# Rounding the high half of each weight tile on the scalar engine instead of on GpSimd, in a two-layer hybrid decoder trunk

## The chip, the cores and the metric

The kernel runs on one core of a Trainium2 chip. The metric is the device time of one execution in microseconds. The engines are named as in the profile: PE (TensorE, the matrix products), PEld (its weight loads), DVE (VectorE), ACT (ScalarE), POOL (GpSimd) and SP (SyncE, which issues the transfers here).

## The reference

Two layers; in each, one input projection feeds three groups of heads (differential attention, dilated attention, a Mamba-2 scan), one output projection joins them, and a gated MLP follows. Everything is float32.

```python
for layer in range(DEPTH):                       # DEPTH = 2, SEQ = 1024, D_MODEL = 1024
    h = rms_norm(x, pre_mix_norm[layer])
    proj = h @ w_in[layer]
    dq, dk, dv, lq, lk, lv, z, xbc, dt = jnp.split(proj, IN_OFFSETS, axis=-1)
    ...
    o_diff = diff_attention(dq, dk, dv, lam, diff_head_norm[layer], lambda_init)
    o_dil = dilated_attention(lq, lk, lv)
    o_ssd = ssd_mixer(z, xbc, dt, ...)
    mix = jnp.concatenate([o_diff, o_dil, o_ssd], axis=-1) @ w_out[layer]
    x = x + rms_norm(mix, post_mix_norm[layer])
    h = rms_norm(x, pre_ffn_norm[layer])
    u = causal_dwconv(h @ ffn_up[layer], ffn_conv_w[layer], ffn_conv_b[layer])
    g, val = jnp.split(u, [D_FF], axis=-1)       # D_FF = 2816
    f = (jax.nn.silu(g) * val) @ ffn_down[layer]
    x = x + rms_norm(f, post_ffn_norm[layer])
```

## The kernel before

Every dense product is made in three passes of a shorter float format (fp32r in the profile). Each operand is split into a high half, the value rounded to that format, and a low half, the rest: hi·hi, hi·lo and lo·hi are added up in one PSUM accumulator. The activations are split once (ah and al, or g for the gated product); the weights are split tile by tile as they come from memory, in `wsplit`: SP loads a tile `wr` of 128x1024 float32 (three buffers; the last, odd piece of a down-projection group is 128x512), one engine writes the rounded copy `wh`, DVE subtracts to get `wl` (four buffers each). So a `wh` can be written when its tile has landed and when the matmuls that read the buffer four tiles earlier are done; `wl` needs `wh`; and `wr` is free for the next load when `wl` is written. There are 390 such tiles in the two layers.

`mm3` (L200 to 211) multiplies weights that stand in the array's place of stationary data (wh, wl) with 512 columns of activations: the parts of the input projection that are wanted transposed, and the FFN's up-projection. `tm3` (L148 to 159), with `tm_units`, has the activations stationary and the weights moving: the rest of the input projection (wtm), the output projection (wout), the down-projection (wdn). Three PSUM accumulators named acc take turns; ACT or DVE empties them (L361 in the causal convolutions, L774 to L777 after wtm, L793 and L794 after wout, L840 and L842 after wdn).

The program goes through each layer in this order: input projection for the first half of the rows with the first attention heads woven in, then for the second half with the rest of the attention and the scan; output projection of the first half; FFN of the first half, with the mixer of the second half woven in; the second half's output projection; its FFN; the norms between. The norm's factor is made in `rstd` (L114 to L123): two small DVE operations, a power on POOL (`rs_r`, L115), and on DVE two or three more (L118 and L119, or L121 to L123); then L243 scales a whole row tile by it. A framework sorts the instructions into each engine's queue by its own estimates of their times and dependencies, with hints from the code (high priority; issue after a given matmul). Each queue then runs in the order so found, and the semaphores between engines follow from the tiles.

Of the kernel before, what the change touches and what calls it, by code (L numbers as in the profile page):

```python
# [13 lines left out]
AF = mybir.ActivationFunctionType  # L14
ALU = mybir.AluOpType
# [54 lines left out]
def body(ctx, tc, x_in, win, wtm, wdt, wout, wup, wdn, cst, gains, dtb, alog, lamp, kst, rope, out):  # L70
    nc = tc.nc
    P = 128
# [6 lines left out]
    V, A, G, T_, Y = nc.vector, nc.scalar, nc.gpsimd, nc.tensor, nc.sync  # L79
# [26 lines left out]
    def fr(ap):  # L106
        return ap.bitcast(F32)
# [17 lines left out]

    xsrc = [x_in[t] for t in range(8)]

    E_ = dict(lo=V)

    def wsplit(src, nk):  # L130
        raw = sp.tile([P, KT * P], F32, tag="wr", bufs=3, name="wr")
        Y.dma_start(raw[:, :nk * P].rearrange("p (a n) -> p a n", a=src.shape[1]) if len(src.shape) == 3 else raw[:, :nk * P], src)
        hi = sp.tile([P, KT * P], F32R, tag="wh", bufs=4, name="wh")
        lo = sp.tile([P, KT * P], F32R, tag="wl", bufs=4, name="wl")
        G.tensor_scalar(hi[:, :nk * P], raw[:, :nk * P], 1.0, 0.0, op0=ALU.mult, op1=ALU.add)  # L135
        E_["lo"].tensor_tensor(lo[:, :nk * P], raw[:, :nk * P], fr(hi[:, :nk * P]), op=ALU.subtract)  # L136
        return hi, lo

    hold = [None]
# [21 lines left out]
    def tm_units(w, k0, nk, pair, evac, before=None, inner=False, pairs=0):  # L161

        def tiles(c):
            return [(i, min(2, nk - i)) + wsplit(w[c, :, k0 + i:k0 + min(i + 2, nk)], min(2, nk - i) * 4)
                    for i in range(0, nk, 2)]
# [132 lines left out]
    for l in range(NL):  # L298
# [118 lines left out]
        def in_unit(name, Ts):  # L417
            hi, lo = wsplit(win[l, IN_IDX[name]], KT)
            for T in Ts:
                a = acc()  # L420
                mm3(a, hi, lo, rhs_of(hT[T]), KT)
                in_evac(name, T, a)
# [379 lines left out]
        def up_pair(T, j, pair):  # L802
            us = []
            for q in range(2):
                jj = j + 22 * q
                hi, lo = wsplit(wup[l, jj], KT)
                a = acc()
                mm3(a, hi, lo, rhs_of(pair), KT)
                u = t2("cv", 4)
                conv(a, u, 3, fw[:, jj], ustate[:, jj], T)  # L810
                us.append(u)
                if q == 0:
                    th = t2("cv", 4)
                    A.activation(th[:], u[:], AF.Tanh)
                    V.scalar_tensor_tensor(u[:], th[:], 1.0, u[:], op0=ALU.add, op1=ALU.mult)
                    yield
            u, w = us
            V.tensor_tensor(u[:], u[:], w[:], op=ALU.mult)
            gh = t2("g", 12, F32R)
            gl = t2("g", 12, F32R)  # L820
            A.activation(gh[:], u[:], AF.Copy)
            V.tensor_tensor(gl[:], u[:], fr(gh[:]), op=ALU.subtract)  # L822
            gt[j] = (gh[:], gl[:])
            yield
# [3 lines left out]
        def down_group(T, gi, fT):  # L828
            k0, n = GROUPS[gi]
            last = gi == len(GROUPS) - 1  # L830
            f = [fT[:, 2 * t:2 * t + 2].rearrange("p k n -> p (k n)") for t in range(4)]
            if last and T:
                xs = load_x(T)
                g3 = load_gain(l, 3)
                g0 = load_gain(l + 1, 0) if l < NL - 1 else None

            def evac(c, t, a):
                d = slice(c * H, (c + 1) * H)
                if gi == 0:
                    A.activation(f[t][:, d], a[:], AF.Copy)  # L840
                else:
                    V.tensor_tensor(f[t][:, d], a[:], f[t][:, d], op=ALU.add)  # L842
                if last and T and l == NL - 1:
                    if c == 0:
                        fin.append((rows(), tiny()))
                    r, sq = fin[-1]
                    A.activation(r[:, d], f[t][:, d], AF.Square, accum_out=sq[:, c:c + 1])
                    if c == 1:
                        V.tensor_tensor(sq[:, 0:1], sq[:, 0:1], sq[:, 1:2], op=ALU.add)
                        rs = rstd(sq[:, 0:1], 1, 1.0 / DM, EPS)  # L850
                        for d in (slice(0, H), slice(H, DM)):
                            V.scalar_tensor_tensor(r[:, d], f[t][:, d], rs[:, 0:1], g3[:, d], op0=ALU.mult, op1=ALU.mult)
                            E = G if d.start == 0 else V
                            E.tensor_tensor(r[:, d], xs[t][:, d], r[:, d], op=ALU.add)
                            Y.dma_start(out[4 * T + t, :, d], r[:, d])
                elif last and T and c == 1:
                    fin.append(fin_norm(4 * T + t, xs[t], f[t], g3, g0))
            return tm_units(wdn[l], k0, n, [gt[k0 + k] for k in range(n)], evac, inner=last and T == 1)
# [108 lines left out]
        dense, rs = out_units(1, pair)  # L967
        run(dense)
        hold[0] = lastmm[0]
        E_["lo"] = V  # L970
        dense = down_group(0, NG - 1, fT0)
        hp = follow(dense, 1, rs, (1, 2, 2, 3))
        run(dense)
        hold[0] = None
        E_["lo"] = V
        fT1 = sp.tile([P, KT, H], F32, tag="act", bufs=4, name="fT")
        dense = ffn(1, hp, fT1)
        half = fin_half(fT0)
# [98 lines left out]
```

## Time and profile before

| | |
|---|---|
| time, median of 3 runs | 2744.13 us (2742.87 to 2744.74) |
| the profiled execution | 2745.8 us, of which its span is 2743.9 |
| granted TensorE clock, mean | 0.988 |
| busy in the span: PE | 2649.0 us (97%) |
| DVE | 1885.0 us (69%) |
| ACT | 883.0 us (32%) |
| POOL | 721.5 us (26%) |
| the copy wh, L135 on POOL | 390 times, 464.4 us |
| the subtraction wl, L136 on DVE | 390 times, 479.1 us |

Busy time is the time in which an instruction of the engine ran; the rest of the span the engine waited. "Idle before" names what ended a wait. [...]

### The profile page before, as it was taken

Reading aid. Unit: us, or ns where it says so; the run is one execution under the profiler, and the core shown is the slowest. Engines: PE = TensorE matmul, PEld = TensorE weight load, DVE = VectorE, ACT = ScalarE, POOL = GpSimd, SP = SyncE. Lnnn points to the kernel's source line nnn. Section 1 sums busy time; section 2 is a strip of 40 time slices with the busy share of each in tenths; the row PEclk is TensorE's granted clock in tenths of the full one; section 3 lists DMA queues with packets and bytes.
Section 4 is the critical chain, followed back from the end, with each engine's and each line's share of the span. In section 5 each row is a group of like instructions: output and inputs, shape, how many; then the busy total and the mean of one; then the engine's idle time right before and its main releaser. Section 6 shows DMA issues by size and latency. Waiting matters only on the chain. (4 is left out here: it accounts for less than half of the span.)

```text
span 2743.9 us, 36451 instructions
## 1 busy us (share of the span) xinstructions
PE 2649.0 (97%) x13160; PEld 2147.8 (78%) x13160; DVE 1885.0 (69%) x3814; ACT 883.0 (32%) x1777; POOL 721.5 (26%) x634
## 2 busy tenths in 40 slices
PE   7999889999999999999999999899999999999998
PEld 6887677888788877888878776778887888788886
DVE  5666867556887686666775677575678775966667
ACT  3252333444432223111223533334444322321111
POOL 2301343232124222222133023332221332322222
PEclk9999999999999999999999999999999999999999
DMA  6653545443333454333257535453434334533332
GB/s 226 216 171 101 180 139 181 119 120 112 104 128 110 130 172 154 96 97 99 88 170 235 152 99 184 125 176 105 126 112 117 119 115 126 200 118 94 100 93 69
DMA packets 157348, 368.83 MB, mean 134 GB/s; under 512 B 18032, under 2 KB 53744, under 8 KB 157168
## 3 DMA queue, kind: packets, MB, share of 16 engines
q1 hardware_dynamic: 157168, 366.49, 42.8%
q8 instruction: 105, 1.72, 0.3%
q14 instruction: 75, 0.61, 0.1%
HBM read 306.13 MB, written 60.29 MB: 134 GB/s over the span
## 5 line engine op out<-in xcount | busy, mean ns | idle before, releaser
L135 POOL TENSOR_SCALAR wh<-wr 128x1024 fp32r<-128x1024 f32 (+1 forms) x390 | 464.4, 1193 | 1390.6 <-PE acc L207 786.8
L204 PE MATMUL acc<-ah,wh 128*128 128x512 f32 x1952 | 776.3, 398 | 1.5 <-ACT ah L255 1.5
L207 PE MATMUL acc<-al,wh 128*128 128x512 f32 x1952 | 765.8, 392 | 0.5 <-DVE al L256 0.5
L208 PE MATMUL acc<-ah,wl 128*128 128x512 f32 x1952 | 764.7, 392 | 0.0
L136 DVE TENSOR_TENSOR wl<-wr,wh 128x1024 fp32r<-128x1024 f32 (+1 forms) x390 | 479.1, 1231 | 251.5 <-POOL wh L135 248.4
L204 PEld LDWEIGHTS acc<-ah,wh 128*128 128x128 f32 x1952 | 368.1, 189 | 82.6 <-issue 10.2
L208 PEld LDWEIGHTS acc<-ah,wl 128*128 128x128 f32 x1952 | 368.1, 189 | 77.4 <-issue 0.5
L207 PEld LDWEIGHTS acc<-al,wh 128*128 128x128 f32 x1952 | 368.1, 189 | 75.1 <-issue 2.7
L363 DVE SCALAR_TENSOR_TENSOR cv<-acc,cs,cv 128x511 f32<-128x511 f32 (+2 forms) x436 | 323.5, 742 | 14.0 <-ACT cv L361 12.2
L154 PE MATMUL acc<-wh,g 128*128 128x512 f32 x704 | 283.1, 403 | 7.6 <-DVE cv L369 6.5
L361 ACT ACTIVATE cv<-acc,cs 128x512 f32<-128x512 f32 x204 | 158.8, 779 | 390.7 <-PE acc L208 379.9
L157 PE MATMUL acc<-wl,g 128*128 128x512 f32 x704 | 276.9, 395 | 6.7 <-DVE wl L136 3.4
L158 PE MATMUL acc<-wh,g 128*128 128x512 f32 x704 | 275.2, 394 | 0.3 <-DVE g L822 0.3
L597 DVE CUSTOM_DVE_ANT_0 P<-s,kc 128x512 f32<-128x512 f32 (+3 forms) x224 | 130.2, 587 | 151.3 <-PE s L595 145.3
L157 PE MATMUL acc<-wl,ah 128*128 128x512 f32 x512 | 208.7, 408 | 16.1 <-DVE wl L136 16.1
L600 ACT ACTIVATE P<-P,tiny 128x128 f32<-128x128 f32 (+7 forms) x224 | 173.3, 774 | 158.4 <-DVE tiny L599 135.3
L154 PE MATMUL acc<-wh,ah 128*128 128x512 f32 x512 | 206.6, 405 | 4.1 <-POOL wh L135 2.4
L158 PE MATMUL acc<-wh,al 128*128 128x512 f32 x512 | 205.9, 402 | 1.8 <-DVE al L256 1.8
L154 PEld LDWEIGHTS acc<-wh,g 128*128 128x128 f32 x704 | 133.1, 189 | 44.7 <-issue 13.1
L157 PEld LDWEIGHTS acc<-wl,g 128*128 128x128 f32 x704 | 133.4, 190 | 33.4 <-DVE wl L136 8.0
L158 PEld LDWEIGHTS acc<-wh,g 128*128 128x128 f32 x704 | 133.3, 189 | 30.0 <-DVE g L822 2.4
L842 DVE TENSOR_TENSOR fT<-acc,fT 128x512 f32<-128x512 f32 x160 | 108.4, 684 | 68.9 <-PE acc L158 68.8
(183 smaller groups left out, 3184.5 us busy)
## 6 DMA issues: line engine op xcount, KB each, us to landing
wr<-in_wup SPq DMA_DIRECT2D x176, 512.0 KB, 3.5
wr<-in_wdn SPq DMA_DIRECT2D x80, 512.0 KB, 3.5
wr<-in_win SPq DMA_DIRECT2D x54, 512.0 KB, 4.4
wr<-in_wtm SPq DMA_DIRECT2D x32, 512.0 KB, 4.9
wr<-in_wout SPq DMA_DIRECT2D x32, 512.0 KB, 4.0
xd<-t SPq DMA_DIRECT2D x24, 512.0 KB, 3.0
t<-xd SPq DMA_DIRECT2D x24, 512.0 KB, 4.3
t<-in_x SPq DMA_DIRECT2D x16, 512.0 KB, 5.4
```

The lines of the kernel that those rows point to most:

```text
L135: G.tensor_scalar(hi[:, :nk * P], raw[:, :nk * P], 1.0, 0.0, op0=ALU.mult, op1=ALU.add)
L136: E_["lo"].tensor_tensor(lo[:, :nk * P], raw[:, :nk * P], fr(hi[:, :nk * P]), op=ALU.subtract)
L154: i = T_.matmul(a[:], xh, hi[:, w], start=(n0 + k == 0), stop=False)
L157: T_.matmul(a[:], xh, lo[:, w], start=False, stop=False)
L158: lastmm[0] = T_.matmul(a[:], xl, hi[:, w], start=False, stop=(n0 + k == n - 1))
L204: i = T_.matmul(a[:], hi[:, w], xh, start=(k == 0), stop=False)
L207: T_.matmul(a[:], hi[:, w], xl, start=False, stop=False)
L208: i = T_.matmul(a[:], lo[:, w], xh, start=False, stop=(k == nk - 1))
L361: A.activation(u[:], a[:], AF.Identity, scale=w[:, n:n + 1], bias=w[:, taps:taps + 1])
L363: V.scalar_tensor_tensor(u[:, d:], a[:, :H - d], w[:, n - d:n - d + 1], u[:, d:], op0=ALU.mult, op1=ALU.add)
L597: V.tensor_tensor_reduce(p[:, c:c + n], s[:, :n], mask[:, o:o + n], 1.0, -1e30 if c == 0 else mx[:, e], ALU.add, ALU.max, mx[:, e])
L600: A.activation(p[:, :nk * P], p[:, :nk * P], AF.Exp, scale=scale, bias=nm[:, e], accum_out=den[:, e])
```

## The change

The copy that rounds a weight tile to `wh` is an activation with the function Copy on ACT instead of a multiply-add by 1 and 0 on POOL. The subtraction goes to DVE by name; before, it went through a small table `E_` that always said DVE. Lines after the table's stand two earlier in the new file (L135 becomes L133, L793 becomes L791), and four earlier at its end.

```diff
-    E_ = dict(lo=V)
-
     def wsplit(src, nk):
...
-        G.tensor_scalar(hi[:, :nk * P], raw[:, :nk * P], 1.0, 0.0, op0=ALU.mult, op1=ALU.add)
-        E_["lo"].tensor_tensor(lo[:, :nk * P], raw[:, :nk * P], fr(hi[:, :nk * P]), op=ALU.subtract)
+        A.activation(hi[:, :nk * P], raw[:, :nk * P], AF.Copy)
+        V.tensor_tensor(lo[:, :nk * P], raw[:, :nk * P], fr(hi[:, :nk * P]), op=ALU.subtract)
         return hi, lo
...
-        E_["lo"] = V
```

The order of the queues follows. On POOL, at the end of the first layer's output projection for the second half of the rows (the stretch around 977 us), the powers of the norms (rs_r) stood between copies. Before:

```order
L115 TENSOR_TENSOR rs_r_8788<-rs_m_8787,kc_69 128x1
L115 TENSOR_TENSOR rs_r_8803<-rs_m_8802,kc_69 128x1
L135 TENSOR_SCALAR wh_8920<-wr_8918 128x1024
L135 TENSOR_SCALAR wh_8926<-wr_8924 128x512
L135 TENSOR_SCALAR wh_9006<-wr_9004 128x1024
L115 TENSOR_TENSOR rs_r_8841<-rs_m_8840,kc_69 128x1
```

Now:

```order
L115 TENSOR_TENSOR rs_r_8788<-rs_m_8787,kc_69 128x1
L115 TENSOR_TENSOR rs_r_8803<-rs_m_8802,kc_69 128x1
L115 TENSOR_TENSOR rs_r_8841<-rs_m_8840,kc_69 128x1
L115 TENSOR_TENSOR rs_r_8856<-rs_m_8855,kc_69 128x1
L115 TENSOR_TENSOR rs_r_8894<-rs_m_8893,kc_69 128x1
```

The three copies have left POOL's row, and nothing has come in their place. On ACT at the same place stand the squares of the norm (P from t4, L240), the evacuations of the output projection (P from acc, L793, and the square of acc, L794) and the halves of the next activations (ah, L255). Before:

```order
L793 ACTIVATE P_8612<-acc_8759 128x512
L794 ACTIVATE acc_8759,tiny_8613<-acc_8759 128x512
L240 ACTIVATE P_8612,tiny_8800<-t4_8676 128x1024
L793 ACTIVATE P_8666<-acc_8812 128x512
L794 ACTIVATE acc_8812,tiny_8667<-acc_8812 128x512
L793 ACTIVATE P_8670<-acc_8865 128x512
L794 ACTIVATE acc_8865,tiny_8671<-acc_8865 128x512
L255 ACTIVATE ah_8941<-tr_8943 128x4x128
L255 ACTIVATE ah_8941<-tr_8950 128x4x128
```

Now:

```order
L791 ACTIVATE P_8612<-acc_8759 128x512
L792 ACTIVATE acc_8759,tiny_8613<-acc_8759 128x512
L238 ACTIVATE P_8612,tiny_8800<-t4_8676 128x1024
L791 ACTIVATE P_8666<-acc_8812 128x512
L792 ACTIVATE acc_8812,tiny_8667<-acc_8812 128x512
L133 ACTIVATE wh_8920<-wr_8918 128x1024
L133 ACTIVATE wh_8926<-wr_8924 128x512
L133 ACTIVATE wh_9006<-wr_9004 128x1024
L791 ACTIVATE P_8670<-acc_8865 128x512
L792 ACTIVATE acc_8865,tiny_8671<-acc_8865 128x512
L133 ACTIVATE wh_9012<-wr_9010 128x512
L253 ACTIVATE ah_8941<-tr_8943 128x4x128
```

Three copies stand ahead of the last evacuation and its square, and a fourth ahead of the ah. At the start of the program, ACT has the squares of the first norms and the first ah. Before:

```order
L240 ACTIVATE P_101,tiny_105<-t4_96 128x1024
L240 ACTIVATE P_102,tiny_120<-t4_118 128x1024
L255 ACTIVATE ah_94<-tr_160 128x4x128
L255 ACTIVATE ah_94<-tr_167 128x4x128
L240 ACTIVATE P_103,tiny_174<-t4_156 128x1024
```

Now:

```order
L238 ACTIVATE P_101,tiny_105<-t4_96 128x1024
L238 ACTIVATE P_102,tiny_120<-t4_118 128x1024
L133 ACTIVATE wh_134<-wr_132 128x1024
L253 ACTIVATE ah_94<-tr_160 128x4x128
L133 ACTIVATE wh_140<-wr_138 128x1024
L253 ACTIVATE ah_94<-tr_167 128x4x128
L133 ACTIVATE wh_146<-wr_144 128x1024
L238 ACTIVATE P_103,tiny_174<-t4_156 128x1024
```

The first copies stand before the first ah and between the two.

## Rows read from the trace of the kernel before

**Rows 1.** The page: busy us of each engine, share, instructions.

```profile
PE 2649.0 (97%) x13160; PEld 2147.8 (78%) x13160; DVE 1885.0 (69%) x3814; ACT 883.0 (32%) x1777; POOL 721.5 (26%) x634
```

**Rows 2.** The page's groups: busy, mean ns of one | idle before, and its releaser.

```profile
L135 POOL TENSOR_SCALAR wh<-wr 128x1024 fp32r<-128x1024 f32 (+1 forms) x390 | 464.4, 1193 | 1390.6 <-PE acc L207 786.8
L136 DVE TENSOR_TENSOR wl<-wr,wh 128x1024 fp32r<-128x1024 f32 (+1 forms) x390 | 479.1, 1231 | 251.5 <-POOL wh L135 248.4
```

**Rows 3.** Windows: length, busy PE, PEld, DVE, ACT, POOL; granted clock, DMA share, GB/s.

```profile
240.00:460.00 220.00, 198.25 (x960) 155.57 (x959) 161.45 (x373) 76.71 (x203) 76.23 (x62) 0.95 0.48 152
960.00:1060.00 100.00, 89.50 (x398) 72.45 (x397) 86.19 (x160) 31.14 (x57) 26.76 (x31) 0.98 0.50 166
1060.00:1360.00 300.00, 299.86 (x1327) 246.26 (x1326) 195.77 (x309) 61.56 (x92) 66.51 (x55) 0.99 0.32 100
1360.00:1420.00 60.00, 55.45 (x248) 44.93 (x247) 46.20 (x71) 14.64 (x28) 16.94 (x18) 0.97 0.53 178
1600.00:1820.00 220.00, 198.45 (x950) 155.56 (x949) 160.96 (x372) 75.51 (x199) 76.25 (x62) 0.95 0.47 150
2330.00:2420.00 90.00, 83.66 (x368) 67.94 (x366) 80.52 (x140) 27.40 (x49) 24.95 (x27) 0.96 0.58 196
...
sum 690.00, PE 625.31 PEld 496.44 DVE 535.32 ACT 225.40 POOL 221.13; mean PE 125.06 PEld 99.29 DVE 107.06 ACT 45.08 POOL 44.23
```

**Rows 4.** Timeline around 978 us: start, length, instruction [idle before <-releaser].

```profile
977.30 2.65 POOL L135 TENSOR_SCALAR wh<-wr 128x1024 fp32r<-128x1024 f32 x3
977.36 1.00 DVE L118 SCALAR_TENSOR_TENSOR rs_q<-rs_r,rs 128x1 f32<-128x1 f32 x1 [0.60 <-POOL rs_r L115]
...
978.39 0.55 DVE L119 SCALAR_TENSOR_TENSOR rs_r<-rs_q,rs_r 128x1 f32<-128x1 f32 x1
...
978.98 2.04 DVE L243 SCALAR_TENSOR_TENSOR P<-t,rs_r,gb 128x1024 f32<-128x1024 f32 x1
...
981.01 1.21 DVE L136 TENSOR_TENSOR wl<-wr,wh 128x1024 fp32r<-128x1024 f32 x1
...
982.28 0.71 PE L157 MATMUL acc<-wl,g 128*128 128x512 f32 x1 [3.38 <-DVE wl L136]
```

**Rows 5.** One line's instructions: ns min/median/max, first and last start.

```profile
L118 DVE SCALAR_TENSOR_TENSOR rs_q<-rs_r,rs x64: 204/220/1076, 6.8 to 2737.1; 128x1 f32<-128x1 f32 x64
...
L119 DVE SCALAR_TENSOR_TENSOR rs_r<-rs_q,rs_r x64: 142/159/992, 7.1 to 2737.4; 128x1 f32<-128x1 f32 x64
...
L243 DVE SCALAR_TENSOR_TENSOR P<-t,rs_r,gb x33: 746/1284/2067, 7.3 to 2364.5; 128x1024 f32<-128x1024 f32 x31, 128x512 f32<-128x512 f32 x2
```

**Rows 6.** Timeline around 440 us: two DVE instructions and the matmul behind them.

```profile
436.37 0.99 DVE L118 SCALAR_TENSOR_TENSOR rs_q<-rs_r,rs 128x1 f32<-128x1 f32 x1 [0.30 <-POOL rs_r L115]
...
438.53 2.07 DVE L243 SCALAR_TENSOR_TENSOR P<-t,rs_r,gb 128x1024 f32<-128x1024 f32 x1
...
443.12 0.79 PE L157 MATMUL acc<-wl,ah 128*128 128x512 f32 x1 [2.78 <-DVE wl L136]
```

**Rows 7.** Timeline of PE: the matmuls behind two other pauses.

```profile
341.43 0.63 PE L684 MATMUL tr<-kc,on 128*128 128x128 f32 x4 [2.05 <-DVE on L679]
...
391.80 0.63 PE L530 MATMUL s<-P,gtr 128*128 128x384 f32 x1 [2.11 <-POOL P L504]
```

**Rows 8.** Timeline of DVE: the first and the last of 66 instructions.

```profile
259.47 1.24 DVE L456 SCALAR_TENSOR_TENSOR dtv<-cv 128x24 f32<-128x24 f32 x1
...
2413.49 1.01 DVE L369 SCALAR_TENSOR_TENSOR cv<-ustate,cs,cv 128x2 f32<-128x2 f32 x1
```

**Rows 9.** Groups by shape, ACT: a square of a 128x1024 tile from SBUF.

```profile
L240 ACT ACTIVATE P<-t 128x1024 f32<-128x1024 f32 x32 | 33.9, 1060 | 58.8 <-DVE t L272 51.5 <-DMA t<-in_x 7.0 <-DVE rs_r L119 0.2
```

**Rows 10.** The five stretches again, L135 alone: 23 + 16 + 10 + 23 + 16 copies.

```profile
240.00:460.00 220.00, 29.38 (x23) 0.95 0.48 152
...
sum 690.00, POOL 105.66; mean POOL 21.13
```

**Rows 11.** Who waited for the loads of wr (us, times), and the part for wup.

```profile
  POOL wh L135: 63.1, 23
...
POOL wh L135 <- DMA wr<-in_wup: 28.1, 8, 14.3
```

More of the change, by code (lines that the diff above doesn't have):

```diff
@@ L974, in body @@
         hold[0] = None
-        E_["lo"] = V
         fT1 = sp.tile([P, KT, H], F32, tag="act", bufs=4, name="fT")
```

## The prediction

> **What bounds the kernel now.** I read the page's line of busy times first [rows 1]: PE is busy 2649.0 us of a span of 2743.9, so some 95 us are all that a faster neighbour can give back, plus what the clock loses. The copy that the change moves is the largest item on POOL [rows 2]: 390 of them, 464.4 us of POOL's 721.5, 1193 ns each. POOL itself is at 26%, so its load is not the point.
>
> Next, the stretches in which PE is not full [rows 3]. The up-projection of the FFN is (299.86 of 300.00 us): nothing done beside it can matter. Five stretches, which hold the attention's and the SSD's ends, the output projections and the changes between norms, are not: of 690.00 us PE is busy 625.31, so 64.7 us lie idle there, two thirds of all there is. [...]
>
> Then the pauses one by one. In the one of 3.38 us before 982.28 [rows 4], PE waits for wl, and wl stands on DVE behind three instructions that took longer than they usually do. While POOL runs three wh copies from 977.30, L118 takes 1.00 us, L119 0.55 and L243 2.04; their medians are 0.22, 0.16 and 1.28 [rows 5]. All three read two tiles in SBUF. L118 starts at 977.36, just behind the copies, and is done at 978.36, which is the length of one copy later. The excess is 0.78 + 0.39 + 0.76 = 1.93 us of the pause's 3.38. The pause of 2.78 us before 443.12 [rows 6] is alike: wl stands behind an L118 of 0.99 and an L243 of 2.07, with an excess of 0.77 + 0.79 = 1.56. The pauses of 2.05 and 2.11 us [rows 7] have no such copy in their chains: the first runs through a slow rs_r of the norm, the other ends on POOL's own P of L504. They stay.
>
> So what the copies cost on POOL is time on DVE, and the change takes POOL out of DVE's way.
>
> **The change, part by part.**
>
> *What goes.* In the four pauses read closely, 1.93 + 1.56 = 3.49 us of 3.38 + 2.78 + 2.05 + 2.11 = 10.32 is hold-up by the copies, 34%. Of 64.7 us that is 22. The other way of counting: for each DVE instruction that overlaps a wh copy I took its time less the tenth percentile of its line and shape. In the five stretches 66 instructions exceed that by over 0.25 us, 48.9 us in all; the first is an L456 of 1.24 us, the last an L369 of 1.01 [rows 8]. About half should lie on PE's path, since the rest is made good while DVE waits for others: 24. I take **-23**. The ends are 0 (DVE runs into the next wait) and -49 (every hold-up counts in full). In the FFN the same hold-ups (L822 beside wh, for instance) cost nothing, because PE is full.
>
> [...]
>
> *The clock.* [...] I take **-4**, ends 0 and -10.
>
> *What comes.* The copy has no row on ACT. The nearest is the square of L240 on ACT, the same 128x1024 from SBUF: 1060 ns [rows 9]. So 390 copies make about 410 us and ACT goes from 883.0 to about 1290 us, 47% of the span: not a bound. In the five stretches there are 88 copies [rows 10], 93 us more on the 225.40 that ACT is busy there. ACT then runs a copy 13% of the time. Any of the 536 ACT instructions of the stretches (203 + 57 + 28 + 199 + 49) meets one with that chance and loses half of 1.06 us: 536 x 0.13 x 0.53 = 37 us, spread over all. Of this a tenth or so, as PE's idle share there (64.7 of 690), falls into chains that PE waits for: 4. I double it for the copies that themselves wait in ACT's queue: **+8**, ends 0 and +37. The order by which the scheduler has put them (the ACT rows shown with the change) sets three of them at the place of [rows 4] between the second and the third evacuation L793, ahead of the two L255 that prepare a next product.
>
> *The start.* There ACT runs the copies between the norms' first operations; the first products need both. **+1**, ends 0 and +2 (two operations of 1.06).
>
> *What moves.* POOL's rs_r (L115) no longer stand behind wh; in the rows shown they follow each other directly. Both were late only by DVE's doing, so I count this at nothing of its own; DVE's wait for rs_r is covered in the -23. The subtraction wl stays on DVE. SP's loads keep their order, and wr is freed by wl as before. The E_ table always said DVE and costs nothing.
>
> *The sum.* The profiled execution took 2745.8 us (1.9 more than its span, 1.7 more than the median of 2744.13). 2745.8 - 23 - 4 + 8 + 1 = 2727.8; less 1.7 that is **2726** beside the median.
>
> **The rivals.**
>
> (1) *No gain.* DVE, set free, only comes earlier to waits that the copies don't make: rs_r, P of L504, the transposes. For it: two of the four pauses [rows 7] are of this kind. Against it: the other two end on a wl that stood in line with nothing else late. Then about -5 is left: 2741 to 2742, within 0.2%.
>
> (2) *Slower, by ACT's queue.* On POOL a waiting copy hurt nobody: it sat 786.8 us for one of its buffer's readers alone [rows 2], and 63.1 us in 23 waits for the transfer of wr [rows 11]. On ACT whatever stands behind it waits too: the evacuations L793 and L361 that free PE's accumulators, the exponentials of L600, the ah of the next product. The buffer waits were foreseen by the scheduler's order, late transfers were not. One of them costs 63.1 / 23 = 2.7 us. To eat up the 18 us of gain, seven of the 23 must fall where PE has no other product; with twelve, 32 us come back and the time is 2758. Against it: most loads are early, and eight of the 23 waits, 28.1 us, were for loads of the up-projection [rows 11], where PE is full. [...]
>
> (3) *The hold-up is not POOL's.* If the copy's reads held DVE up from whichever engine, -23 and -4 fall away and +9 stays: 2753. Against it: L118's end fits the end of one copy on POOL [rows 4].
>
> **How the numbers follow.** Forecast 0.68, (1) 0.15, (2) 0.13, (3) 0.04. What a measurement of this kernel can tell from no change is about 0.2%, 5.5 us: the forecast is faster, (1) the same, (2) and (3) slower. The forecast's own range goes to -36 for the hold-up (half way to its end) with no price on ACT, 2744 - 36 - 4 + 1 = 2705, and upward into (1). The whole range goes further up to 2752, short of (2) and (3) in full: 2705 to 2752.
>
> **What would show it.** POOL's line falls to about 257 us, ACT's rises to about 1290, with 390 copies of about 1.06 us. L118, L119 and L243 on DVE fall to means near their medians; wl's mean falls below its 1231 ns. The five stretches, by the same work and not by the same clock time, have less PE idle: about 40 us instead of 64.7. If the step is wrong, DVE's means fall and PE's idle time stays (rival 1), or PE's waits end on ACT's evacuations with a wh before them that waits for wr (rival 2), or the DVE means don't fall (rival 3). A start that is late by more than 2 us would be a mis-sized term only.

## The result: faster by 46 us, and more than was forecast

The changed kernel takes 2697.8 us (median of four runs, 2694.39 to 2698.24) against 2743.5 of the kernel before in the same comparison: a ratio of 0.9834, with a 95% interval of 0.9817 to 0.9851. The forecast was 2726 with a range from 2705: the sign and the place were right, the size was less than half of what came. The medians leave out one execution of one kernel below, which ran at a granted clock of 0.568 and took 4368.56 us.

The page of the changed kernel first: busy times, and the copy and the subtraction, which answer to [rows 1] and [rows 2].

```profile
PE 2625.3 (97%) x13160; PEld 2135.6 (79%) x13160; DVE 1830.1 (68%) x3814; ACT 1246.8 (46%) x2167; POOL 252.4 (9%) x244
...
L134 DVE TENSOR_TENSOR wl<-wr,wh 128x1024 fp32r<-128x1024 f32 (+1 forms) x390 | 470.5, 1209 | 264.1 <-ACT wh L133 259.8
L133 ACT ACTIVATE wh<-wr 128x1024 fp32r<-128x1024 f32 (+1 forms) x390 | 403.9, 1040 | 432.9 <-PE acc L205 254.4
```

POOL lost 469 us of work and ACT took 364 (its instructions overlap by some 0.1 us, since the copies alone make 403.9: the one that starts at 966.71 takes 1.05 us, and the next instruction starts at 967.66). The span is 2695.8 us, so PE is idle for 2695.8 - 2625.3 = 70.5 us instead of 94.9. Its busy time fell by 23.7 us too, although it does the same 13160 matmuls. Most of that is the clock, whose mean rose from 0.988 to 0.994: what it misses of 1, times the span, was 32.9 us and is 16.2, so 16.7 less. The other 7 us are not explained. In the trace's record of the granted clock, a share of the full one, stand two levels, 1.0 and 0.5; the lower one comes 16 times in the kernel before and 9 times in the changed one, 12 and 8 of them for 3.4 us each.

The five stretches of [rows 3], now. The windows below hold the same matmuls (found by counting them from the start), not the same times. Columns: length, busy time of PE, PEld, DVE, ACT and POOL with instruction counts, granted clock, DMA share, GB/s.

```profile
239.10:444.70 205.60, 192.70 (x960) 152.10 (x960) 148.64 (x373) 99.00 (x226) 46.29 (x39) 0.98 0.51 164
947.90:1042.00 94.10, 87.92 (x397) 71.21 (x396) 80.28 (x162) 46.59 (x75) 9.59 (x15) 1.00 0.56 185
1341.70:1396.60 54.90, 53.46 (x248) 44.03 (x247) 39.97 (x71) 24.44 (x38) 5.38 (x8) 1.00 0.56 192
1574.50:1777.10 202.60, 189.76 (x950) 150.13 (x949) 148.15 (x372) 97.72 (x222) 46.02 (x39) 0.98 0.51 164
2287.40:2373.00 85.60, 82.01 (x367) 66.63 (x366) 73.61 (x140) 42.10 (x65) 7.97 (x11) 0.98 0.60 206
sum 642.80, PE 605.85 PEld 484.11 DVE 490.65 ACT 309.84 POOL 115.26; mean PE 121.17 PEld 96.82 DVE 98.13 ACT 61.97 POOL 23.05
```

They took 690.00 us and take 642.80: 47.2 us of the 48.1 by which the span fell. PE's idle time in them went from 64.7 to 37.0, by 27.7 us. The clock's missing parts times the lengths made 11.0 + 2.0 + 1.8 + 11.0 + 3.6 = 29.4 us and now make 4.1 + 0 + 0 + 4.1 + 1.7 = 9.9, by 19.5 less. PE's busy time in them fell from 625.31 to 605.85, by 19.5 us as well, for the same matmuls; so here the clock explains what the pauses don't. 27.7 + 19.5 = 47.2: pauses and clock together are the whole gain, three parts to two.

One pause as it was and is. This is the timeline around the first pause read closely, [rows 4], in the changed kernel: start, length, engine, line, instruction, and in brackets the idle time before it.

```profile
964.52 0.55 POOL L115 TENSOR_TENSOR rs_r<-rs_m,kc 128x1 f32<-128x1 f32 x1 [4.54 <-DVE rs L116]
...
965.11 0.22 DVE L118 SCALAR_TENSOR_TENSOR rs_q<-rs_r,rs 128x1 f32<-128x1 f32 x1 [0.61 <-POOL rs_r L115]
...
965.24 2.52 ACT L133 ACTIVATE wh<-wr 128x1024 fp32r<-128x1024 f32 x3
...
965.36 0.16 DVE L119 SCALAR_TENSOR_TENSOR rs_r<-rs_q,rs_r 128x1 f32<-128x1 f32 x1
...
965.56 1.28 DVE L241 SCALAR_TENSOR_TENSOR P<-t,rs_r,gb 128x1024 f32<-128x1024 f32 x1
...
967.08 1.22 DVE L134 TENSOR_TENSOR wl<-wr,wh 128x1024 fp32r<-128x1024 f32 x1
...
968.35 0.50 PE L155 MATMUL acc<-wl,g 128*128 128x512 f32 x1 [1.51 <-DVE wl L134]
```

The three copies run at the same place, now on ACT, for 2.52 us. Beside them L118 takes 0.22 us (it took 1.00), L119 0.16 (0.55) and L241, the former L243, 1.28 (2.04). The pause is 1.51 us instead of 3.38: shorter by 1.87, where the prediction had counted 1.93 of hold-up. Over the whole kernel no L118 is late any more:

```profile
L118 DVE SCALAR_TENSOR_TENSOR rs_q<-rs_r,rs x64: 209/220/223, 6.7 to 2689.3; 128x1 f32<-128x1 f32 x64
```

Its longest is 223 ns, against 1076 in [rows 5].

### The profile page after: what moved, and what is told of

It reads as the page before. It is cut to its first block, busy times and chain, and to the rows that moved or that the text cites. A ratio compares the mean times of both kernels' runs of the same rounds, so it can differ in the third digit from the quotient of the medians.

```text
span 2695.8 us, 36379 instructions
## 1 busy us (share of the span) xinstructions
PE 2625.3 (97%) x13160; PEld 2135.6 (79%) x13160; DVE 1830.1 (68%) x3814; ACT 1246.8 (46%) x2167; POOL 252.4 (9%) x244
## 5 line engine op out<-in xcount | busy, mean ns | idle before, releaser
L134 DVE TENSOR_TENSOR wl<-wr,wh 128x1024 fp32r<-128x1024 f32 (+1 forms) x390 | 470.5, 1209 | 264.1 <-ACT wh L133 259.8
L133 ACT ACTIVATE wh<-wr 128x1024 fp32r<-128x1024 f32 (+1 forms) x390 | 403.9, 1040 | 432.9 <-PE acc L205 254.4
L115 POOL TENSOR_TENSOR rs_r<-rs_m,kc 128x1 f32<-128x1 f32 (+2 forms) x88 | 66.0, 754 | 1337.6 <-DVE rs L116 1326.8
```

What stands on the lines that cost most here:

```text
L133: A.activation(hi[:, :nk * P], raw[:, :nk * P], AF.Copy)
L134: V.tensor_tensor(lo[:, :nk * P], raw[:, :nk * P], fr(hi[:, :nk * P]), op=ALU.subtract)
```

## Experiments: does POOL's reading do it?

Theory A is the prediction's: an instruction on DVE with two inputs in SBUF waits while POOL reads SBUF for the copy; PE pauses behind it, and the clock falls behind the pause. Theory B: the gain comes from POOL's queue, in which powers and other work stood behind copies. Theory C: it comes from the order that the scheduler found this time, and from the shorter copy (a mean of 1040 ns against 1193). Two kernels tell them apart. Both keep the copy on ACT and give POOL 390 needless instructions that write the wl buffer before DVE does. In one they read wr, in the other they read nothing. The orders of the DVE instructions of these two are nearly the same (3797 of 3814 stand in the same order).

```diff
-        A.activation(hi[:, :nk * P], raw[:, :nk * P], AF.Copy)
+        A.activation(hi[:, :nk * P], raw[:, :nk * P], AF.Copy); G.tensor_scalar(lo[:, :nk * P], raw[:, :nk * P], 1.0, 0.0, op0=ALU.mult, op1=ALU.add)
```

> The changed kernel (copy on ACT), and beside it POOL copies the same wr tile with the old multiply-add into the wl buffer, which DVE then overwrites: POOL reads SBUF again as often and as long as before, but nothing that wh needs goes through POOL. Theory A (POOL's reads hold DVE's two-input instructions up, PE's pauses follow and the clock falls behind the pauses): 2730 to 2748 us, PE idle back to about 90 us, mean clock 0.988, L118's mean above 300 ns. Theory B (what was won is POOL's queue, in which rs_r and others stood behind wh): about 2740 too, but then the same for the next kernel, which fills POOL without reading. Theory C (the order that the scheduler found, and the shorter copy, 1058 against 1217 ns): within 5 us of 2698.

And the one that only writes:

```diff
-        A.activation(hi[:, :nk * P], raw[:, :nk * P], AF.Copy)
+        A.activation(hi[:, :nk * P], raw[:, :nk * P], AF.Copy); G.memset(fr(lo[:, :nk * P]), 0.0)
```

> The changed kernel, and beside it POOL writes zeros into the wl buffer before DVE overwrites it: the same number of POOL instructions of the same size at the same places, in front of the same rs_r, but they read nothing. Theory A: 2695 to 2706 us (a few us at the start, where four of them stand before the first rs_r), L118's mean near 220 ns, mean clock 0.993. Theory B: as the kernel whose POOL reads, some 2740. Theory C: 2698.

The first took 2738.09 us (0.998 of before, 0.9971 to 0.9989), the second 2689.06 (0.9804, 0.9789 to 0.9819): 49 us apart. First the kernel whose POOL reads: the page's line of busy times,

```profile
PE 2642.5 (96%) x13160; PEld 2143.6 (78%) x13160; DVE 1906.3 (70%) x3814; ACT 1243.1 (45%) x2167; POOL 719.1 (26%) x634
```

and the views of two lines, POOL's needless instructions and L118 (ns min/median/max):

```profile
L133 POOL TENSOR_SCALAR wl<-wr x390: 618/1056/2125, 10.7 to 2711.3; 128x1024 fp32r<-128x1024 f32 x187, 128x512 fp32r<-128x512 f32 x8
...
L118 DVE SCALAR_TENSOR_TENSOR rs_q<-rs_r,rs x64: 203/220/1019, 8.5 to 2732.1; 128x1 f32<-128x1 f32 x64
```

Then the kernel whose POOL only writes, its busy times,

```profile
PE 2621.8 (98%) x13160; PEld 2133.8 (79%) x13160; DVE 1829.3 (68%) x3814; ACT 1245.9 (46%) x2167; POOL 618.2 (23%) x634
```

and the same two lines:

```profile
L133 POOL MEMSET wl<- x390: 522/956/969, 0.7 to 2661.6; 128x1024 f32 x187, 128x512 f32 x8
...
L118 DVE SCALAR_TENSOR_TENSOR rs_q<-rs_r,rs x64: 206/219/222, 12.2 to 2682.5; 128x1 f32<-128x1 f32 x64
```

POOL is nearly as full in both, with as many instructions in front of the same powers. Where it reads, DVE is busy 77 us longer for the same work, L118 takes up to 1019 ns, PE is idle 96.4 us and the time is within 0.2% of the old one. Where it only writes, nothing of this happens. That speaks for A and against the other two: B asks for the same time in both, C for 2698 in both. (The second kernel came out 6 us below the range expected of it, see the end.) So beside POOL instructions that only write L118 is not held up: 222 ns at most, against 1019.

How long is one hold-up? The same kernel as the first, with POOL reading only half the columns:

```diff
-G.tensor_scalar(lo[:, :nk * P], raw[:, :nk * P], 1.0, 0.0, op0=ALU.mult, op1=ALU.add)
+G.tensor_scalar(lo[:, :nk * H // 8], raw[:, :nk * H // 8], 1.0, 0.0, op0=ALU.mult, op1=ALU.add)
```

> As the kernel in which POOL copies each wr tile into the wl buffer beside ACT, but only the first half of its columns: POOL reads as often, half as long. If a DVE instruction with two SBUF inputs waits for the whole of POOL's instruction, the hold-ups are half as long: L118's longest near 0.7 us instead of 1.02, and the time between the two kernels of that pair, 2705 to 2722 (2689 with none, 2738 with all). If any read of POOL, short or long, costs the same, 2730 to 2740.

It took 2720.14 us (0.9911, 0.9896 to 0.9926), and its L118 and POOL rows (ns min/median/max) are

```profile
L118 DVE SCALAR_TENSOR_TENSOR rs_q<-rs_r,rs x64: 206/220/620, 7.0 to 2711.8; 128x1 f32<-128x1 f32 x64
...
L133 POOL TENSOR_SCALAR wl<-wr x390: 404/622/2035, 9.9 to 2690.7; 128x512 fp32r<-128x512 f32 x187, 128x256 fp32r<-128x256 f32 x8
```

The median of POOL's instruction fell from 1056 to 622 ns, to 59%; of the 49 us 31 are left, 63%; the longest L118 is 620 ns, about one such instruction. The two shares prove little by being alike. DVE's busy time fell further, from 77 us above that of the kernel whose POOL only writes to 21 (1850.3 against 1829.3), and this kernel's DVE order differs from the pair's in some 120 places of 3814. What shows the length is the single hold-up, here the longest L118 and what POOL ran beside it:

```profile
1378.06 0.62 POOL L133 TENSOR_SCALAR wl<-wr 128x512 fp32r<-128x512 f32 x1
1378.06 0.62 DVE L118 SCALAR_TENSOR_TENSOR rs_q<-rs_r,rs 128x1 f32<-128x1 f32 x1 [0.44 <-POOL rs_r L115]
```

L118 stands beside POOL's instruction and ends with it. So do all L118 and L119 of over 300 ns: each ends within 10 ns of the end of a POOL instruction that reads a wr tile, 21 of them in the kernel before, 21 where POOL reads the whole tile, 15 where it reads half. In the changed kernel and where POOL only writes there is none. The hold-up lasts until the POOL instruction beside it is done.

One more rival has to go. In the kernels of the pair DVE's subtraction must also wait until POOL has written the wl buffer: 158.8 us in 132 waits where POOL reads, 142.1 us in 113 where it doesn't. Perhaps the first is slow by these waits alone. With half the columns they are 41.3 us in 53, less than in either, and still that kernel is 31 us slower than the one that only writes. They are not the cause.

## Experiments: where the copies cost

Half of the cut each: first all copies on ACT but the up-projection's, then only the up-projection's.

```diff
-    def wsplit(src, nk):
+    def wsplit(src, nk, on_act=True):
...
-        A.activation(hi[:, :nk * P], raw[:, :nk * P], AF.Copy)
+        A.activation(hi[:, :nk * P], raw[:, :nk * P], AF.Copy) if on_act else G.tensor_scalar(hi[:, :nk * P], raw[:, :nk * P], 1.0, 0.0, op0=ALU.mult, op1=ALU.add)
...
-                hi, lo = wsplit(wup[l, jj], KT)
+                hi, lo = wsplit(wup[l, jj], KT, False)
```

> Of the changed kernel only the copies of the up-projection's weights (176 of 390) go back to POOL. If hold-ups in the FFN cost nothing, since PE is full there, 2696 to 2704 us. If they matter (the first half's FFN has the second half's mixer woven in), 2710 to 2720, in proportion to their share of 45%.

The second is the same with the two values of `on_act` exchanged.

> The other half of the same cut: the up-projection's copies on ACT, the other 214 on POOL as before. If the gain sits in the five stretches, 2736 to 2744 us, about the kernel before; if it is in proportion to the copies moved, 2720 to 2726.

They took 2703.8 us (0.9858, 0.9843 to 0.9872) and 2732.82 (0.9965, 0.9951 to 0.9978), with 2742.67 for the kernel before beside them: gains of 39 and 10 us, which add up to about the whole. So 45% of the copies bring a fifth of the gain, since PE is full where most of them run. But it is not nothing, as the prediction said of the FFN; the second kernel missed its expectation by 3 us. The 10 us don't lie where PE is full: by the same matmuls, the full stretch of [rows 3] takes 299.6 us in the kernel before, 299.2 in the changed one and 300.0 in this one, while the five stretches together are 13.7 us shorter than before. Part of this may be the order, which changes with every such cut; this was not taken apart.

## Experiments: what the clock gives back, and what ACT pays

To price the clock by itself, the changed kernel got more work on DVE in the chains that PE waits for, with nothing on POOL: the norm's scaling L241 done twice, whole or by half.

```diff
-            V.scalar_tensor_tensor(r[:, d], xt[:, d], rs[:, 0:1], gb[:, d], op0=ALU.mult, op1=ALU.mult)
+            V.scalar_tensor_tensor(r[:, d], xt[:, d], rs[:, 0:1], gb[:, d], op0=ALU.mult, op1=ALU.mult); (None if halves else V.scalar_tensor_tensor(r[:, d], xt[:, d], rs[:, 0:1], gb[:, d], op0=ALU.mult, op1=ALU.mult))
```

> The changed kernel with the norm's scaling (L241, 128x1024, 1.28 us on DVE) done twice, 31 times: 40 us of DVE work put into the chains that PE waits for, with nothing added on POOL. It asks what a us of PE's pause costs in all. If the prediction's clock term was right (4 us of clock for 23 us of pause), the time grows by about 1.2 times what PE's idle time grows. If the clock gives back as much as the runs so far suggest (17 us of clock for 24 of pause between the two kernels), by 1.5 to 1.8 times, with the mean clock falling from 0.994 to 0.991 or less. Time 2715 to 2735 either way.

```diff
-            V.scalar_tensor_tensor(r[:, d], xt[:, d], rs[:, 0:1], gb[:, d], op0=ALU.mult, op1=ALU.mult)
+            V.scalar_tensor_tensor(r[:, d], xt[:, d], rs[:, 0:1], gb[:, d], op0=ALU.mult, op1=ALU.mult); (None if halves else V.scalar_tensor_tensor(r[:, :H], xt[:, :H], rs[:, 0:1], gb[:, :H], op0=ALU.mult, op1=ALU.mult))
```

> The same with half the dose: 512 of the 1024 columns done twice, some 0.7 us, 22 us of DVE in all. If a longer pause costs more clock in proportion, half of the other's loss, 2706 to 2716. If short pauses are free of it, the time grows by the idle time alone, some 5 to 10 us, and the mean clock stays at 0.993 to 0.994.

2717.53 us (0.9907, 0.989 to 0.9924) and 2709.49 (0.988, 0.9864 to 0.9896), both in the ranges expected, the second in that of a clock which pays in proportion to the pause (2706 to 2716). To see what the added time is, the profiled executions of all twelve kernels side by side, those of the next section too; idle is the span less PE's busy time, lost is the span times what the mean clock misses of 1 (given to three digits, so good to some 1.4 us), rest is what is left of the span:

| kernel | span | PE idle | clock | lost | rest |
|---|---|---|---|---|---|
| before | 2743.9 | 94.9 | 0.988 | 32.9 | 2616 |
| changed | 2695.8 | 70.5 | 0.994 | 16.2 | 2609 |
| POOL reads beside | 2738.9 | 96.4 | 0.988 | 32.9 | 2610 |
| POOL writes beside | 2689.0 | 67.2 | 0.995 | 13.4 | 2608 |
| POOL reads half beside | 2719.5 | 86.1 | 0.991 | 24.5 | 2609 |
| up-projection's copies on POOL | 2700.6 | 74.8 | 0.995 | 13.5 | 2612 |
| only those on ACT | 2727.2 | 87.6 | 0.991 | 24.5 | 2615 |
| scaling twice | 2716.7 | 81.3 | 0.990 | 27.2 | 2608 |
| scaling one and a half times | 2707.5 | 76.5 | 0.992 | 21.7 | 2609 |
| copied twice on ACT | 2701.7 | 69.5 | 0.992 | 21.6 | 2611 |
| less on POOL | 2680.5 | 61.9 | 0.997 | 8.0 | 2611 |
| only powers on POOL | 2680.6 | 59.8 | 0.997 | 8.0 | 2613 |

Against the changed kernel the full dose adds 10.8 us of idle time and 11.0 of clock, the half dose 6.0 and 5.5. So here a us that PE pauses costs nearly two. Elsewhere it costs less: between the pair of kernels above lie 29.2 us of idle time and 19.5 of clock, between the changed kernel and the one whose POOL reads half 15.6 and 8.3. Two kernels don't follow at all: with the up-projection's copies on POOL PE is idle 4.3 us more than in the changed kernel and 2.7 less are lost, and with everything copied twice on ACT it is the other way round. Each row is one execution, and one kernel's clock differs between executions (0.990 to 0.993 with the scaling done twice). So the price of a us of pause is one and a half to two, and not sharper than that.

The records show it at the pause from above. In the kernel before, behind the 3.38 us, the matmuls take 0.63 us and follow each other at 0.42 to 0.43, half the pace of the higher level:

```profile
982.79 0.63 PE L158 MATMUL acc<-wh,g 128*128 128x512 f32 x1
983.21 0.63 PE L154 MATMUL acc<-wh,g 128*128 128x512 f32 x1
983.64 0.63 PE L157 MATMUL acc<-wl,g 128*128 128x512 f32 x1
```

In the changed kernel, behind the 1.51 us, they take 0.39 to 0.40 and follow at 0.23:

```profile
968.68 0.39 PE L156 MATMUL acc<-wh,g 128*128 128x512 f32 x1
968.91 0.40 PE L152 MATMUL acc<-wh,g 128*128 128x512 f32 x1
969.14 0.40 PE L155 MATMUL acc<-wl,g 128*128 128x512 f32 x1
```

Not every pause of one length is alike: behind a pause of 2.11 us that remains in the changed kernel the low level still comes,

```profile
379.93 0.44 PE L528 MATMUL s<-P,gtr 128*128 128x384 f32 x1 [2.11 <-POOL P L502]
...
381.13 0.63 PE L156 MATMUL acc<-wh,al 128*128 128x512 f32 x1
```

while behind the one of 2.06 us that ends at 334.04 they go on at 0.22 to 0.24 us. So a rule by the pause's length alone doesn't follow from these runs.

ACT's price was put at +8 us. Its test is a second copy of each tile on ACT:

```diff
-        A.activation(hi[:, :nk * P], raw[:, :nk * P], AF.Copy)
+        A.activation(lo[:, :nk * P], raw[:, :nk * P], AF.Copy); A.activation(hi[:, :nk * P], raw[:, :nk * P], AF.Copy)
```

> The changed kernel with each weight tile copied twice on ACT, once into the wl buffer (which DVE overwrites) and once into wh: ACT's added work a second time, about 1650 us busy. The prediction charged +8 us for the first 390 copies. If that was right, the second costs as much or somewhat more: 2706 to 2714. If ACT's copies are hidden altogether, 2694 to 2702. If a waiting copy in ACT's queue is what hurts, 2720 and more, with PE's waits ending on ACT's evacuations.

2703.08 us (0.9861, 0.9841 to 0.9881), 5 us above the changed kernel, with intervals that overlap; it lies between the ranges expected of copies that are hidden (to 2702) and of the price charged (from 2706). ACT is now busy 1584.9 us, 59%. A price between 0 and 8 us can't be told apart further by this; 20 us and more is excluded. And it is the second copy's price, not that of the first.

## An experiment with the rest of POOL's work

If A holds, POOL's other instructions do the same harm. The low halves of the rotary products and one of two decay masks go to DVE, the scaling of the second half's probabilities to ACT.

```diff
-                    G.tensor_tensor(lo[:], q[:], fr(h[:]), op=ALU.subtract)
+                    V.tensor_tensor(lo[:], q[:], fr(h[:]), op=ALU.subtract)
...
-                for x, at, E in ((ahi[T][:, c * 6:c * 6 + 6], ath, G), (col(5, c), atl, V)):
+                for x, at, E in ((ahi[T][:, c * 6:c * 6 + 6], ath, V), (col(5, c), atl, V)):
...
-                        (A.activation(p0[:, :w], p0[:, :w], AF.Copy, scale=cf[:, e]) if T == 0 else G.tensor_scalar(p0[:, :w], p0[:, :w], cf[:, e], 0.0, op0=ALU.mult, op1=ALU.add))
+                        A.activation(p0[:, :w], p0[:, :w], AF.Copy, scale=cf[:, e])
```

> The changed kernel with more of POOL's work taken off it: the low halves of the rotary products (L404, 40 times) and one of the two decay masks (L502, 16) go to DVE, the scaling of the second half's probabilities (L711, 48) to ACT. In the changed kernel 49 us of DVE's time are still hold-ups beside these. If the prediction's mechanism holds for them and half lies on PE's path, -20 us with clock; DVE pays 27 + 15 us of own work for it. Expected 2680 to 2695; if DVE's added work eats the gain, 2695 to 2705.

2681.28 us, a ratio of 0.9775 (0.9759 to 0.9791): the fastest of all, clear of the changed kernel's interval. DVE's busy time did not grow, although 56 instructions came to it. L404 and L502 take 38 us more of it in sum, and eight other lines, L813 and L717 first, take 32 us less, as they would if hold-ups had left them:

```profile
PE 2618.6 (98%) x13160; PEld 2133.1 (80%) x13160; DVE 1829.5 (68%) x3870; ACT 1288.4 (48%) x2215; POOL 117.6 (4%) x140
```

Not all of the gain is hold-up, though. PE's idle time fell by 8.6 us, and 4 of them are the two pauses that ended on POOL's P of L502: the mask now comes from DVE, which is quicker at it (1163 against 2016 ns), and they are 0.28 and 0.22 us where they were 2.11 and 2.09.

Taking the scan's last POOL work and half of the last additions away as well, so that only the powers stay:

```diff
-                    G.tensor_tensor(y[:], y[:], ys[:], op=ALU.add)
+                    V.tensor_tensor(y[:], y[:], ys[:], op=ALU.add)
...
-                            E = G if d.start == 0 else V
+                            E = V
```

(L510 and L564 as the first, which is L548; the second is L851.)

> The kernel with less on POOL (2681 us), and the scan's remaining POOL work (L510, L548, L564) and the last additions (L851) on DVE too: POOL keeps the powers rs_r alone. There are 13 us of hold-ups left beside these; DVE pays about 0.5 us more for each of 44 instructions. Expected 2674 to 2684: no more than 5 us either way.

2684.04 us (0.9783, 0.9766 to 0.9799): no further gain, and at the upper end of what was expected. POOL had only 117.6 us of work left before this step, and DVE's busy time went up by 5.5, to 1835.0: what DVE gets back is less than what it takes on.

## Why the prediction was right about the cause and wrong about the size

**What bounds, and where.** Right. The five stretches hold 47.2 of the 48.1 us. The FFN was given 0; its copies bring at most 10, and none of that in the stretch where PE is full.

**The hold-ups, -23, with ACT's price, +8.** Too small a gain by 12.7. Idle time in the five stretches fell by 27.7, against 23 - 8 = 15. The gross term is what the pair of kernels measures: 27.0 us of idle time in the five stretches (59.2 where POOL reads, 32.2 where it only writes), where the prediction's two ways gave 22 and 24. So the hold-ups were 4 us too small, and the mechanism of this term was right. The way there held some luck: the four pauses read closely were to lose 3.49 us and lost 2.07 (they went from 10.32 to 1.51 + 2.57 + 2.06 + 2.11 = 8.25), while others went by more. Three of these before:

```profile
287.57 0.30 PE L735 MATMUL tr<-kc,P 128*128 128x128 f32 x1 [2.19 <-DVE tiny L599]
...
310.83 0.44 PE L595 MATMUL s<-k,Q 128*128 128x384 f32 x1 [2.02 <-DVE tiny L597]
...
365.94 0.48 PE L485 MATMUL tr<-kc,yq 128*128 128x128 f32 x1 [3.36 <-ACT yq L577]
```

The first two are gone in the changed kernel, and the third is 1.12 us. The pause that was 2.78 us long, in the changed kernel:

```profile
427.54 0.50 PE L155 MATMUL acc<-wl,ah 128*128 128x512 f32 x1 [2.57 <-DVE wl L134]
```

It still ends on wl, and the pause of 2.11 us shown above on POOL's P. The price on ACT is the other part of the miss, and the larger: 8 us were charged, and nothing of it shows, since the net fall of 27.7 us is no less than the gross of 27.0. A second copy on ACT cost some 5 us, and none of it as idle time of PE (69.5 us against 70.5).

**The clock, -4.** The step that failed, and the largest miss. No run shows the 4: the five stretches got 19.5 us back, and behind the pause that shrank from 3.38 to 1.51 us no low clock comes at all. The end of -10 is about a third of the 29.4 us that the clock lost there, as the hold-ups are a third of the pauses read closely; two thirds went. The lower end of the range held the clock at -4 as well (2744 - 36 - 4 + 1 = 2705). Its -36 for the hold-ups had room for the 27.7 us of idle time; with 19.5 for the clock it would have been 2689.5.

**The sum.** 12.7 us of idle time and 15.5 of clock missed make 28.2, the distance from 2726 to 2697.8. That it fits to the tenth is chance: between the profiled executions 48.1 us came where the sum had 18, so 30.1 were missed, 1.9 of them outside the five stretches.

**The start, +1.** The first 250 matmuls take some half a us longer. Right in size.

**The rivals.** Rival 1's own time was wrong (5 us off 2744 are 2739, not 2741 to 2742), and it was half right about single pauses: the two without a copy in their chains stayed as they were (2.06 and 2.11), and the one before 443.12 became only 0.21 us shorter, since al and other norms stand in DVE's line before wl there. It did not decide. Rival 2 did not come: the changed kernel's ACT waited 30.9 us in 19 waits for wr, half of what POOL had waited [rows 11], and PE's weight loads in `tm3` waited 4.1 us in all for a wh from ACT. That what stands behind a waiting copy waits too shows once at the place read closely: the copy at 971.77 had waited 2.93 us for its wr, and the two ah behind it start at 972.31, though the transposes that they read (eight from 970.30, 1.03 us) were done before the copy started. It cost nothing there, since PE ran on with other products, one every 0.22 to 0.23 us. Rival 3 is excluded by L118's 223 ns, its longest with all copies on ACT.

**What stays open.** The kernel in which POOL only writes is 9 us faster than the changed one, though it does more. Its order of instructions differs, and why it is faster stays open. So differences of this size between kernels with different orders don't prove a cause. The pair that carries the verdict has nearly one order and is 49 us apart.

## What to carry to other kernels

Before giving POOL work because it is idle, look at what DVE runs beside it: here L118 and L119, DVE instructions with two inputs in SBUF, lasted until POOL's instruction beside them was done (to within 10 ns) when that one read SBUF, and between the two kernels whose POOL reads and only writes this cost 49 us, because DVE was on PE's path. A 0.22 us instruction that sometimes takes 1.0 is the mark of it in a trace (compare the minimum, the median and the maximum of one line). And price a pause of PE by time and clock together: here each us taken out of the pauses gave back some half to one us more from the clock.

## What was not expected of the hardware

The clock's return is as large as that: over most kernels of the table, idle time and lost clock fall together, from 94.9 and 32.9 us to 59.8 and 8.0, while the rest of the span stays within 2608 to 2616 us. And an instruction of 0.22 us on one column of 128 values is held as well as one on a whole tile: in the kernel before L118 took up to 1076 ns and L243 up to 2067, with medians of 220 and 1284 [rows 5].
